# Fixing the order of weight splits and sums, and moving four steps, in the squared-ReLU MLP of an fp32 encoder layer

## The chip, the cores and the metric

The kernel runs on one core of a Trainium2 chip, as one program. The metric is the device time of one execution in microseconds; the median of three runs is 1119.77 us (1118.83 to 1120.58). The core has five engines with a queue each, which the profile names PE (TensorE; PEld is its weight load), DVE (VectorE), ACT (ScalarE), POOL (GpSimd) and SP (SyncE, which issues the transfers here).

## What is computed

One encoder layer in float32 for 256 tokens of width 2048: a mixer of two attention kinds, a cross attention over 256 memory tokens, and an MLP of width 8192, each followed by a layer norm of `alpha*x + f(x)`. The change touches only the MLP:

```python
def squared_relu_mlp(h, w_mlp_in, w_mlp_out):
    return jnp.square(jax.nn.relu(h @ w_mlp_in)) @ w_mlp_out
...
        ff = squared_relu_mlp(x, w_mlp_in[l], w_mlp_out[l])
        x = layer_norm(ALPHA * x + ff, ln3_g[l], ln3_b[l])
```

## The kernel before

**Products in three parts.** Every float32 operand is split in a high part, which TensorE's fast float32 form holds, and a low part, the remainder. `split` (L85) writes the high part with a ScalarE copy (L87) and the low part with a VectorE subtraction (L88). A product is then three matmuls (`mm3`, L152 to L155): high by high, high by low, low by high.

**The MLP in chunks.** The 8192 hidden columns are cut into NCH = 4 chunks of CH = 16 column tiles of 128. Chunk 0 of the hidden layer is made in four groups of four tiles (`hidden_group`, L944). From there on a mixed part runs: while the second product of chunk c goes on, the hidden columns of chunk c + 1 are made. The second product of a chunk goes in two halves q = 0, 1 of 1024 output columns, so there are eight passes (c, q), `PASSES` in the code, run by `one_pass` (L1011).

**Items.** The mixed part is a hand-written list `items` (L880 to L892) of two kinds. A tile item ("g", c + 1, j) makes one hidden column tile (`hidden_tile`, L965): two weight pieces of 1024 columns are split, 16 matmuls of 512 columns (L973) and 16 of 256 (L981) fill one PSUM bank, `evacuate` (L856) brings it to SBUF (ScalarE L858, VectorE L859), and after each second tile `finish` (L861) does relu and square (L863, L864), splits the pair, and for pairs 2 to 7 (`SEVEN`) forms four sums of its quarters (L874) and splits them too. A unit item ("u", c, q, p) multiplies hidden pair p (two blocks of 128 tokens by two of 128 hidden columns) with its 256 x 1024 piece of the output weights. In each half with q = 0 the first FIRST = 6 tiles stand one ahead of each of the first six units; with q = 1 the other ten stand one ahead of each unit and two ahead of each of the last two. The last chunk has units only.

**Sevens and plain units.** A plain unit takes eight block products into the four sum banks x11, x12, x21, x22. A seven takes seven products, some of sums of blocks, into x11, x12, x21 and the product banks p1, p5, p6, p7. It needs three sums of weight pieces on VectorE (`push_sums`, L913; the instructions are of L919), which go to the buffer s_t and are split from there. `SEVENS` and `ORDER` (L821 to L824) say which pairs of a pass are sevens and in which order the units go. In the last chunk's first half they are 4 to 7 of (0, 4, 1, 5, 2, 6, 3, 7), in its last half 5, 6, 7 of (0, 5, 6, 1, 7, 2, 3, 4). PSUM has eight banks and all are in use: the x banks are the page's "acc", the p banks its "att".

**Merges.** When a pass has done its last seven, p1 is copied to m_t (L1075), and eight VectorE steps (L1038, L1036 in the first chunk, and L1041) that merge the products into the residual `res` are put in `banks`; each weight piece then takes one of them off (`pump`), and the first seven of the next pass takes all that are left. The x banks are merged at the end of the pass. A tile ahead of a pass's first unit writes bank p6 (x22 in the first pass), tiles between the sevens write x22, tiles after them p1 and p7.

**Order of the work.** `part` (L925) splits one weight piece and then takes one sum, or else one side job, off its queue. The program is built by a tile framework that orders each engine's instructions itself, from an estimate of the time line (`schedule_with_timeline_sim=True`, L1270); program order is a guide, and only what `pin` (L82) marks keeps it. Weights come by SyncE in tiles of 1024 KB into four buffers in turn (`fetch`, L894, issue L908), one fetch at the start of each item. Split weights go to four high buffers and four low buffers.

**The end.** The last three units of the last pass (HELD = 3) first fill x12 and x11 for token block 0; their splits are kept and later serve block 1 in x21 and, in two quarters, two product banks. `done` (L1110) adds the banks to the residual and takes statistics; the layer norm of block 0, then block 1, follows on VectorE (L1145, L1153) with the output transfers (L1156).

Of the kernel before, what the change touches and what calls it, by code (L numbers as in the profile page):

```python
# [14 lines left out]
AF = mybir.ActivationFunctionType  # L15
ALU = mybir.AluOpType
# [17 lines left out]
CH = 16  # L34
# [4 lines left out]
def encoder_kernel(ctx: ExitStack, tc: tile.TileContext, t, out):  # L39
    nc = tc.nc  # L40
# [20 lines left out]
    def f(ap):  # L61
        return ap.bitcast(F32)
# [22 lines left out]
    def split(hi, lo, src, scale=None, pinned=False):  # L85
        if scale is None:
            pin(nc.scalar.activation(hi, src, AF.Copy), pinned)  # L87
            return pin(nc.vector.tensor_tensor(out=lo, in0=src, in1=f(hi), op=ALU.subtract), pinned)  # L88
        else:
            nc.scalar.activation(hi, src, AF.Copy, scale=scale)  # L90
            nc.vector.scalar_tensor_tensor(
                out=lo, in0=src, scalar=scale, in1=f(hi), op0=ALU.mult, op1=ALU.subtract)
# [7 lines left out]
        return r[:, :n]  # L100

    side, banks, fixed_lo = deque(), deque(), deque()

    def pump(n=1):

# [205 lines left out]
    class Heads:  # L311
# [11 lines left out]
        def finish(self):  # L323
            while self.live:
                self.step()
# [495 lines left out]
    ORDER = {cq: (2, 3, 4, 5, 6, 7, 0, 1) for cq in PASSES[:-2]}  # L821
    SEVENS = {cq: SEVEN for cq in PASSES[:-2]}
    ORDER[NCH - 1, 0], SEVENS[NCH - 1, 0] = (0, 4, 1, 5, 2, 6, 3, 7), (4, 5, 6, 7)
    ORDER[NCH - 1, 1], SEVENS[NCH - 1, 1] = (0, 5, 6, 1, 7, 2, 3, 4), (5, 6, 7)  # L824
    HELD = 3
    FIRST = 6
    s_in = Stream(t["w_mi"][4:])
    sts = [stats_tile() for _ in range(NB)]
    ht = big3("ht")
# [16 lines left out]
    def give(what, c, p):  # L846
        free[what].append(place[what, c, p])
# [31 lines left out]
    raws, raw_of, fetched, sums = [raw_x], {}, [0], deque()  # L879
    items = []  # L880
    for c, q in PASSES:
        gs = [("g", c + 1, j) for j in range(CH)] if c < NCH - 1 else []
        gs = gs[:FIRST] if q == 0 else gs[FIRST:]
        us = [("u", c, q, p) for p in ORDER[c, q]]
        n = len(gs) - len(us)
        for i, u in enumerate(us):
            twice = i >= len(us) - n if n > 0 else False
            for _ in range(2 if twice else 1):
                if gs:
                    items.append(gs.pop(0))  # L890
            items.append(u)
        assert not gs  # L892

    def fetch():  # L894

        n = fetched[0]
        if n == len(items):
            return
        it = items[n]
        fetched[0] += 1  # L900
        if n and n < 4:
            raws.append(raw_tile())
        raw = raw_of[it] = raws[n % 4]
        if it[0] == "g":
            src = t["w_mc"][(it[1] - 1) * CH + it[2]]
        else:
            src = t["w_mo"][(it[1] * 2 + it[2]) * (CH // 2) + it[3]]
        nc.sync.dma_start(raw, src)  # L908
# [4 lines left out]
    def push_sums(it):  # L913

        raw = raw_of[it]
        b12, b22, b21 = [raw[:, o:o + 512] for o in (0, 1024, 1536)]

        def add(out, a, b):
            sums.append(lambda: nc.vector.tensor_tensor(out=out, in0=a, in1=b, op=ALU.add))  # L919
        add(s_t[:, 0:1024].rearrange("p (i c) -> p i c", i=2), raw[:, 512:1536].rearrange("p (i c) -> p i c", i=2),  # L920
            b12[:, None, :].broadcast_to([P, 2, 512]))
        add(s_t[:, 1024:1536], s_t[:, 0:512], b22)
        add(s_t[:, 1536:2048], s_t[:, 1024:1536], b21)

    def part(src, hi=None, lo=None):  # L925
        w = src.shape[1]
        if hi is None:
            hi = wsp.tile([P, 1024], F32R, tag="w_hi", name="w_hi")
        if lo is None:
            lo = lo_tile()  # L930
        split(hi[:, :w], lo[:, :w], src)
        if banks:
            pump()
        if sums:
            sums.popleft()()
        else:
            pump()
        return hi[:, :w], lo[:, :w]
# [21 lines left out]
                evacuate(outs[i + j], l, h, j)  # L960
            finish(h, c, (j0 + i) // 2)

    lh = []

    def hidden_tile(it, ps):  # L965

        _, c, j = it
        for h_ in range(2):
            hi, lo = part(raw_of[it][:, h_ * 1024:(h_ + 1) * 1024])
            k0 = 8 * h_  # L970

            def w_hi(k):
                nc.tensor.matmul(ps, hi[:, k * P:(k + 1) * P], x2t[:, k0 + k, :],  # L973
                                 start=k0 + k == 0, stop=k0 + k == KT - 1)

            for k in range(7):
                w_hi(k)
            if h_ == 0:
                w_hi(7)
            for k in range(8):  # L980
                nc.tensor.matmul(ps[:, 0:S], lo[:, k * P:(k + 1) * P], x2t[:, k0 + k, 0:S],  # L981
                                 start=False, stop=False)
            if h_ == 1:
                w_hi(7)
        if j % 2 == 0:
            lh[:] = [tmp_tile(), tmp_tile()]
        evacuate(ps, *lh, j % 2)
        if j % 2:
            finish(lh[1], c, j // 2)

    bank = []
    at = [0]
# [1 line left out]
    def step():  # L994

        it = items[at[0]]
        at[0] += 1
        fetch()
        if at[0] < len(items) and not is_seven(it) and is_seven(items[at[0]]):
            push_sums(items[at[0]])  # L1000
        return it
# [9 lines left out]
    def one_pass(c, q):  # L1011
# [32 lines left out]
        while n_unit < len(order):  # L1044
            it = step()
            if it[0] == "g":
                if n_unit == 0:
                    ps = x22 if (c, q) == (0, 0) else p6
                elif n_seven < len(sevens):
                    ps = x22  # L1050
                else:
                    spare = spare or [p1, p7]
                    ps = spare[0]
                    spare.reverse()
                hidden_tile(it, ps)
                continue
            p, raw, k = it[3], raw_of[it], 2 * it[3]
            n_unit += 1
            if p in sevens:
                if n_seven == 0:  # L1060
                    while banks:
                        banks.popleft()()
                while sums:
                    sums.popleft()()
                for src, todo in ((raw[:, 512:1536], ((p1, a(c, k, 0)), (x12, sm(c, p, 3)))),
                                  (raw[:, 1536:2048], ((x11, a(c, k + 1, 0)),)),
                                  (s_t[:, 0:1024], ((p5, sm(c, p, 0)), (p7, sm(c, p, 2)))),
                                  (s_t[:, 1024:2048], ((p6, sm(c, p, 1)), (x21, a(c, k + 1, 1))))):
                    for (hi, lo), (ps, x) in zip(halves(part(src)), todo):
                        mm(ps, x, hi, lo)  # L1070
                n_seven += 1
                if at[0] < len(items) and is_seven(items[at[0]]):
                    push_sums(items[at[0]])
                if n_seven == len(sevens):
                    nc.scalar.activation(m_t, p1, AF.Copy)  # L1075

                    banks.extend([lambda: merge(r11, m_t), lambda: more(p6),
                                  lambda: merge(r12, m_t, ALU.subtract), lambda: more(p7),
                                  lambda: merge(r21, m_t), lambda: merge(r22, m_t, ALU.subtract),
                                  lambda: merge(r22, p5), lambda: merge(r12, p5)])  # L1080
            elif final and len(order) - n_unit < HELD:
                n = len(parts) // 2
                for i in range(2):
                    o = (2 * n + i) * 1024
                    lo = wide[:, 6144 + o:7168 + o] if n == 0 else aux[:, 2048 + o:3072 + o]
                    w = halves(part(raw[:, i * 1024:(i + 1) * 1024], wide[:, o:o + 1024], lo))
                    parts.append((k + i, w))
                    for (hi, lo), ps in zip(w, (x12, x11)):
                        mm(ps, a(c, k + i, 0), hi, lo)
            else:  # L1090
                for i in range(2):
                    w = halves(part(raw[:, i * 1024:(i + 1) * 1024]))
                    for (hi, lo), to in zip(w, ((x12, x22), (x11, x21))):
                        for b in range(2):
                            mm(to[b], a(c, k + i, b), hi, lo)
            if q == 1:
                give("h", c, p)
                if p in SEVEN:
                    give("s", c, p)
        if not final:  # L1100
            for r, ps in ((r22, x22), (r12, x12), (r11, x11), (r21, x21)):
                merge(r, ps)
            if c == NCH - 1:
                banks.extend([lambda b=b, r=r: stats(sts[b], r)
                              for b, r in ((0, r11), (0, r12), (1, r21), (1, r22))])
            return
# [167 lines left out]
```

## Time and profile before

| what | value |
|---|---|
| median of three runs | 1119.77 us |
| the profiled execution's own time | 1118.91 us |
| its span, first to last instruction | 1117.1 us |
| TensorE (PE) busy | 1085.0 us, 5855 matmuls |
| VectorE (DVE) busy | 949.0 us, 1344 instructions |
| ScalarE (ACT) busy | 641.6 us, 928 instructions |
| mean granted TensorE clock | 0.991 |
| read from HBM | 212.78 MB |

A row of the timeline reads: start in us from the span's start, duration, engine, source line, operation, tile written and tiles read, shapes, count, and in brackets the idle time before it with what ended it. A row of the stretches has its length, then each engine's busy time with its count of instructions, the granted clock (1.00 is full), the DMA engines' busy share and GB/s. In a row of waits stand the total, the count and the longest. In a row of groups stand the busy time, the mean duration in ns and the idle time before. The mixed part begins near 494 us with the first tile item, its last pass ends near 1101 us, and the final normalisation ends the kernel.

### The profile page before, as it was taken

The page shows a single profiled execution, that of the slowest core. Times are in us where ns is not written, and L with a number is a line of the kernel's source. Part 1 is how long each engine was busy: PE and PEld are TensorE (multiplying, and loading weights), DVE is VectorE, ACT ScalarE, POOL GpSimd, SP SyncE. Part 2 cuts the span into 40 slices and gives each one's busy share as a digit, 9 for nine tenths or more (in the row PEclk, how much of TensorE's full clock was granted, in tenths as well). Part 3 has the DMA queues.
Part 4 walks back from the last instruction along what each step waited for, and adds up shares of the span by engine and source line. Part 5 has one row for each costly group of instructions (what it writes and reads, how often), then busy time and mean ns, then how long its engine had stood idle before and what let it go on. Part 6 is the DMA issues. An engine that isn't in the chain of part 4 may idle for free.

```text
span 1117.1 us, 15372 instructions
## 1 busy us (share of the span) xinstructions
PE 1085.0 (97%) x5855; PEld 930.1 (83%) x5855; DVE 949.0 (85%) x1344; ACT 641.6 (57%) x928; POOL 38.2 (3%) x45
## 2 busy tenths in 40 slices
PE   9999999999999999999999999999999999999984
PEld 6988899888998878887878888878888878888763
DVE  5878677687888777898899988899989989988988
ACT  6555566546576345576657656566655655755540
POOL 1402000000100000000000000000000000000000
PEclk9999999999999999999999999999999999999987
DMA  9664454466477426654545655546565455564532
GB/s 327 234 226 151 152 189 141 162 226 238 177 226 263 153 76 226 221 195 158 219 177 200 219 196 188 219 159 226 188 212 192 182 205 190 188 226 170 207 140 87
DMA packets 37945, 215.87 MB, mean 193 GB/s; under 512 B 4336, under 2 KB 5232, under 8 KB 14192
## 3 DMA queue, kind: packets, MB, share of 16 engines
q1 hardware_dynamic: 37872, 214.89, 53.9%
q8 instruction: 46, 0.75, 0.3%
q14 instruction: 27, 0.22, 0.1%
HBM read 212.78 MB, written 2.10 MB: 192 GB/s over the span
## 4 chain that ended last, share of the span: by engine, by line
PE 88%; DVE 6%; DMA 2%; ACT 1%; issue 1%; SPq 0%; POOL 0%; DVEq 0%; ACTq 0%
PE acc L154 12%; PE acc L155 12%; PE acc L153 12%; PE acc L973 9%; PE att L973 6%; PE acc L981 5%; PE att L153 4%; PE att L154 4%; PE att L155 4%; PE att L981 3%; PE acc L202 3%; PE att L202 3%; PE acc L195 2%; PE acc L193 2%; PE acc L194 2%; DVE lo L88 2%
## 5 line engine op out<-in xcount | busy, mean ns | idle before, releaser
L87 ACT ACTIVATE w_hi<-raw 128x1024 fp32r<-128x1024 f32 (+2 forms) x320 | 305.1, 970 | 160.8 <-PE acc L155 90.3
L88 DVE TENSOR_TENSOR lo<-raw,w_hi 128x1024 fp32r<-128x1024 f32 (+1 forms) x190 | 206.5, 1101 | 8.7 <-ACT w_hi L87 7.7
L88 DVE TENSOR_TENSOR w_lo<-raw,w_hi 128x1024 fp32r<-128x1024 f32 (+2 forms) x130 | 146.0, 1132 | 59.2 <-ACT w_hi L87 58.2
L973 PE MATMUL acc<-x2t,w_hi 128*128 128x512 f32 x496 | 129.0, 392 | 0.2 <-DVE tmp L859 0.2
L88 DVE TENSOR_TENSOR lo<-s_t,w_hi 128x1024 fp32r<-128x1024 f32 x86 | 104.9, 1221 | 18.4 <-ACT w_hi L87 13.2
L87 ACT ACTIVATE w_hi<-s_t 128x1024 fp32r<-128x1024 f32 x86 | 90.7, 1056 | 42.5 <-PE acc L155 24.6
L973 PEld LDWEIGHTS acc<-x2t,w_hi 128*128 128x128 f32 x496 | 91.0, 189 | 17.5 <-ACT w_hi L87 0.6
L973 PE MATMUL att<-x2t,w_hi 128*128 128x512 f32 x272 | 70.4, 393 | 1.3 <-DVE m_t L1041 1.3
L981 PEld LDWEIGHTS acc<-x2t,lo 128*128 128x128 f32 x496 | 67.6, 190 | 4.7
L858 ACT ACTIVATE tmp<-acc 128x256 f32<-128x256 f32 x39 | 14.4, 384 | 97.5 <-PE acc L973 94.6
L154 PE MATMUL acc<-w_lo,xt 128*128 128x512 f32 (+2 forms) x192 | 69.6, 364 | 0.1
L155 PE MATMUL acc<-w_hi,xt 128*128 128x512 f32 (+2 forms) x192 | 69.6, 363 | 0.0
L981 PE MATMUL acc<-x2t,lo 128*128 128x256 f32 x496 | 69.1, 282 | 0.0
L88 DVE TENSOR_TENSOR lo<-raw_x,w_hi 128x1024 fp32r<-128x1024 f32 (+1 forms) x56 | 66.7, 1209 | 2.7 <-ACT w_hi L87 2.6
L153 PE MATMUL acc<-w_hi,xt 128*128 128x512 f32 (+2 forms) x192 | 66.3, 365 | 0.9 <-ACT w_hi L87 0.9
L154 PE MATMUL acc<-lo,ht 128*128 128x512 f32 x158 | 62.0, 392 | 2.4 <-DVE lo L88 2.4
L155 PE MATMUL acc<-w_hi,ht 128*128 128x512 f32 x158 | 61.6, 390 | 0.0
L87 ACT ACTIVATE w_hi<-raw_x 128x1024 fp32r<-128x1024 f32 (+1 forms) x56 | 57.4, 1046 | 4.8 <-PE att L973 1.5
L973 PEld LDWEIGHTS att<-x2t,w_hi 128*128 128x128 f32 x272 | 49.6, 189 | 11.4 <-DVE m_t L1041 2.7
L919 DVE TENSOR_TENSOR s_t<-s_t,raw 128x512 f32<-128x512 f32 x84 | 57.4, 684 | 0.1
L153 PE MATMUL acc<-w_hi,ht 128*128 128x512 f32 x158 | 54.9, 396 | 0.3 <-ACT w_hi L87 0.3
L919 DVE TENSOR_TENSOR s_t<-raw 128x1024 f32<-128x1024 f32 x42 | 51.3, 1222 | 1.5 <-DMA raw<-in_w_mo 0.8
(308 smaller groups left out, 2513.7 us busy)
## 6 DMA issues: line engine op xcount, KB each, us to landing
raw<-in_w_mo SPq DMA_DIRECT2D x54, 1024.0 KB, 4.9
raw<-in_w_mc SPq DMA_DIRECT2D x30, 1024.0 KB, 4.8
raw_x<-in_w_mc SPq DMA_DIRECT2D x18, 1024.0 KB, 4.9
raw<-in_w_out SPq DMA_DIRECT2D x16, 1024.0 KB, 4.9
raw<-in_w_mi SPq DMA_DIRECT2D x16, 1024.0 KB, 4.9
raw_x<-in_w_mo SPq DMA_DIRECT2D x10, 1024.0 KB, 4.9
raw<-in_w_b SPq DMA_DIRECT2D x5, 1024.0 KB, 4.9
raw<-in_w_qa SPq DMA_DIRECT2D x16, 256.0 KB, 5.4
```

Of the source, the lines that this page charges most:

```text
L87: pin(nc.scalar.activation(hi, src, AF.Copy), pinned)
L88: return pin(nc.vector.tensor_tensor(out=lo, in0=src, in1=f(hi), op=ALU.subtract), pinned)
L153: nc.tensor.matmul(ps, ah, bh, start=start, stop=False)
L154: nc.tensor.matmul(ps, ah, bl, start=False, stop=False)
L155: nc.tensor.matmul(ps, al, bh, start=False, stop=stop)
L193: nc.tensor.matmul(ps, hi, xt[:, k, 0:S], start=k == 0, stop=False)
L194: nc.tensor.matmul(ps, hi, xt[:, k, S:2 * S], start=False, stop=False)
L195: nc.tensor.matmul(ps, lo, xt[:, k, 0:S], start=False, stop=k == nk - 1)
L202: pin(nc.tensor.matmul(ps, hi[:, i * P:(i + 1) * P], xt[:, k, :], start=k == 0, stop=k == nk - 1), pinned)
L919: sums.append(lambda: nc.vector.tensor_tensor(out=out, in0=a, in1=b, op=ALU.add))
L973: nc.tensor.matmul(ps, hi[:, k * P:(k + 1) * P], x2t[:, k0 + k, :], start=k0 + k == 0, stop=k0 + k == KT - 1)
L981: nc.tensor.matmul(ps[:, 0:S], lo[:, k * P:(k + 1) * P], x2t[:, k0 + k, 0:S], start=False, stop=False)
```

## The change

Five edits, all in the mixed part.

- **Queued.** Each w_hi copy, each low subtraction of `part` and each sum of `push_sums` gets an order dependence on the one queued before it on the same engine. ScalarE so keeps program order among its weight copies, VectorE among its weight subtractions and sums. No semaphore is added; evacuations, finishes and merges are not queued.
- **Last half all plain.** The pass (3, 1) takes its eight units in order 0 to 7, none of them a seven.
- **Two tiles lead.** In the first pass (0, 0) two tile items stand ahead of the first unit, and seven instead of six in that pass; nine are left for (0, 1). The second tile writes p6.
- **Finish later.** The finish of a tile pair is put behind the next unit, or ahead of the next tile if that comes first.
- The construction of `items` is rewritten for this; from (1, 0) to (2, 1) it gives the same list as before.

```diff
+    queued = {}
+
+    def queue(ins):
+
+        i = ins.ins
+        if i.engine in queued:
+            tc.add_manual_dep(i, queued[i.engine], mybir.DependencyInfo(
+                mybir.DependencyClass.NoSync, mybir.DependencyReason.DATA), reason="queue")
+        queued[i.engine] = i.name
+        return ins
...
-    ORDER[NCH - 1, 1], SEVENS[NCH - 1, 1] = (0, 5, 6, 1, 7, 2, 3, 4), (5, 6, 7)
+    ORDER[NCH - 1, 1], SEVENS[NCH - 1, 1] = tuple(range(CH // 2)), ()
     HELD = 3
-    FIRST = 6
...
     for c, q in PASSES:
-        gs = [("g", c + 1, j) for j in range(CH)] if c < NCH - 1 else []
-        gs = gs[:FIRST] if q == 0 else gs[FIRST:]
         us = [("u", c, q, p) for p in ORDER[c, q]]
-        n = len(gs) - len(us)
+        if c == NCH - 1:
+            items += us
+            continue
+        lead = 7 if c == 0 else 6
+        gs = [("g", c + 1, j) for j in (range(lead, CH) if q else range(lead))]
+        twice = range(8 - (len(gs) - 8), 8) if q else range(lead - 6)
         for i, u in enumerate(us):
-            twice = i >= len(us) - n if n > 0 else False
-            for _ in range(2 if twice else 1):
-                if gs:
-                    items.append(gs.pop(0))
-            items.append(u)
-        assert not gs
+            n = 2 if i in twice else 1
+            items += gs[:n] + [u]
+            gs = gs[n:]
...
         def add(out, a, b):
-            sums.append(lambda: nc.vector.tensor_tensor(out=out, in0=a, in1=b, op=ALU.add))
+            sums.append(lambda: queue(nc.vector.tensor_tensor(out=out, in0=a, in1=b, op=ALU.add)))
...
-        split(hi[:, :w], lo[:, :w], src)
+        queue(nc.scalar.activation(hi[:, :w], src, AF.Copy))
+        queue(nc.vector.tensor_tensor(out=lo[:, :w], in0=src, in1=f(hi[:, :w]), op=ALU.subtract))
...
-    lh = []
+    lh, late_finish = [], []
...
         if j % 2:
-            finish(lh[1], c, j // 2)
+            late_finish.append(lambda h=lh[1]: finish(h, c, j // 2))
...
         at[0] += 1
+        if it[0] == "g" and late_finish:
+            late_finish.pop()()
         fetch()
...
                 if n_unit == 0:
-                    ps = x22 if (c, q) == (0, 0) else p6
+                    ps = x22 if it[1:] == (1, 0) else p6
...
                 if p in SEVEN:
                     give("s", c, p)
+            if late_finish:
+                late_finish.pop()()
```

## The prediction

> **What bounds the kernel now.** I read the page first, then the busy time by stretches, then the timeline of the mixed MLP part (from about 494 us on).
>
> ```profile
> span 1117.1 us, 15372 instructions
> ...
> PE 1085.0 (97%) x5855; PEld 930.1 (83%) x5855; DVE 949.0 (85%) x1344; ACT 641.6 (57%) x928; POOL 38.2 (3%) x45
> ...
> PE 88%; DVE 6%; DMA 2%; ACT 1%; issue 1%; SPq 0%; POOL 0%; DVEq 0%; ACTq 0%
> ```
>
> TensorE is busy nearly all the time and carries 88% of the chain that ended last. So a gain can only be TensorE work that goes or TensorE idle time that goes, and the change adds TensorE work. The busy time of each stretch (columns: length, PE, PEld, DVE, ACT, POOL, clock, DMA share, GB/s) says where there is idle time to win:
>
> ```profile
> 554.30:640.00 85.70, 84.46 (x422) 70.71 (x420) 82.20 (x109) 55.54 (x72) 0.00 (x0) 1.00 0.55 195
> 640.00:724.80 84.80, 84.80 (x440) 72.88 (x441) 75.75 (x94) 49.78 (x64) 0.00 (x0) 1.00 0.56 201
> ...
> 1063.50:1101.00 37.50, 32.70 (x148) 26.78 (x148) 32.11 (x42) 10.82 (x12) 0.00 (x0) 0.91 0.32 112
> ```
>
> From 640.0 to 724.8 TensorE never rests; the stretch before loses a little, with VectorE at 82.20 of 85.70; the end loses much, and there the clock fell to 0.91. Busy time hides part of a loss, because the end of a matmul is modelled, so I count starts. The pitch of a 512-column matmul at full rate comes from two starts that are 21 matmuls apart:
>
> ```profile
> 1005.04 0.39 PE L155 MATMUL acc<-w_hi,ht 128*128 128x512 f32 x1
> ...
> 1009.80 0.39 PE L155 MATMUL acc<-w_hi,ht 128*128 128x512 f32 x1
> ```
>
> 4.76 / 21 = 0.227 us. What lies beyond 0.227 per matmul is lost.
>
> **Last half all plain.** In the last half (3, 1) the three pairs 5, 6, 7 went by seven products and now go by eight. The loss there before:
>
> ```profile
> 1057.20:1074.30 17.10, 11.48 (x35) 0.80 0.31 116
> ```
>
> ```profile
> 1063.54 0.49 PE L153 MATMUL att<-w_hi,aux 128*128 128x512 f32 x1
> 1064.04 2.35 DVE L88 TENSOR_TENSOR wide<-raw,wide 128x1024 fp32r<-128x1024 f32 x2
> ...
> 1067.52 1.26 DVE L1038 TENSOR_TENSOR res<-res,att 128x512 f32<-128x512 f32 x2
> ...
> 1068.84 0.79 PE L153 MATMUL att<-w_hi,aux 128*128 128x512 f32 x1 [4.80 <-DVE res L1038]
> ...
> 1073.00 0.63 PE L154 MATMUL att<-lo,aux 128*128 128x512 f32 x1
> ...
> 1073.43 0.63 PE L155 MATMUL att<-w_hi,aux 128*128 128x512 f32 x1
> ```
>
> The first window row is TensorE alone: 35 matmuls in 17.10 us, where 35 x 0.227 = 7.9 would do: 9.2 us lost. Most of it is one wait: a seven-product of the last half needs the product banks (p1, p5, p6, p7, "att") that the previous half filled, and VectorE merges them into the residual (L1038) only after low parts of later units. After this idle time the pitch is 0.43 (1073.00 to 1073.43) instead of 0.227, and the window's clock is 0.80. [...]
>
> Plain units touch no product bank, so this wait has no cause left: -9.2. Price: a plain unit has 8 x 3 matmuls, a seven 7 x 3, so 3 x 3 x 0.227 = +2.0. What is late next is the merge of the four sum banks (x22, x12, x11, x21) at the boundary of the halves, which the plain units do need. Four such merges, two to 1.26 us by the row above, are 2.5; the last seven hides most of it, since x22 and x12 are finished before its last matmuls; I take +0.5 (bounds 0 and 2.5). The merges of the products now lie behind the plain units, and VectorE has room for them: the change takes these off it,
>
> ```profile
> L919 DVE TENSOR_TENSOR s_t<-s_t,raw 128x512 f32<-128x512 f32 x84 | 57.4, 684 | 0.1
> ...
> L919 DVE TENSOR_TENSOR s_t<-raw 128x1024 f32<-128x1024 f32 x42 | 51.3, 1222 | 1.5 <-DMA raw<-in_w_mo 0.8
> ```
>
> 3 x (2 x 0.68 + 1.22) = 7.7 us of sums, beside the splits of those sums and eight merges. Transfers: 1 MB per plain unit of 24 x 0.227 = 5.4 us is 193 GB/s (w_mo tiles are 1024 KB), and 640.0 to 724.8 moved 201 GB/s without a rest of TensorE; nothing. Together -6.7.
>
> **Splits and sums queued.** All w_hi copies on ScalarE, and all lo subtractions and sums (L919) on VectorE, now keep program order. What that repairs:
>
> ```profile
> 899.42 1.07 PE L153 MATMUL acc<-w_hi,ht 128*128 128x512 f32 x4
> 899.48 1.23 DVE L919 TENSOR_TENSOR s_t<-raw 128x1024 f32<-128x1024 f32 x1 [0.77 <-DMA raw<-in_w_mo]
> ...
> 900.62 1.22 DVE L88 TENSOR_TENSOR lo<-raw_x,w_hi 128x1024 fp32r<-128x1024 f32 x1
> ...
> 901.90 0.50 PE L154 MATMUL acc<-lo,ht 128*128 128x512 f32 x1 [1.41 <-DVE lo L88]
> ...
> 902.24 0.40 PE L155 MATMUL acc<-w_hi,ht 128*128 128x512 f32 x1
> ```
>
> A sum for the next half's first seven stands on VectorE ahead of the lo that TensorE needs at once, and even waits for its transfer. Four matmuls from 899.42 would let the next start at 900.33; it starts at 901.90, and the one after it comes 0.34 later instead of 0.227: 1.57 + 0.11 = 1.68 lost, 0.27 more than the idle time in brackets. The same pattern, shorter, stands at three places:
>
> ```profile
> 515.94 0.50 PE L154 MATMUL att<-lo,aux 128*128 128x512 f32 x1 [0.55 <-DVE lo L88]
> ```
>
> ```profile
> 560.03 0.50 PE L154 MATMUL acc<-lo,ht 128*128 128x512 f32 x1 [0.55 <-DVE lo L88]
> ```
>
> ```profile
> 730.53 0.50 PE L154 MATMUL acc<-lo,aux 128*128 128x512 f32 x1 [0.55 <-DVE lo L88]
> ```
>
> Each 0.55 + 0.27 = 0.82. In program order the sum comes behind the next tile's first lo: 1.68 + 3 x 0.82 = -4.1.
>
> The cost of a fixed order: where the lo at the head waits for its w_hi, a sum that was ready used to fill VectorE, and now stands behind it with every later lo; TensorE waits for those. What VectorE waits for in one chunk (554.3 to 724.8):
>
> ```profile
> DVE tmp L859 <- ACT tmp L858: 6.2, 6, 1.8
> DVE lo L88 <- ACT w_hi L87: 5.4, 13, 0.5
> ```
>
> Lower bound 0: merges, evacuations and finishes aren't queued and fill the hole, and the postponed finish (below) gives more of that. Upper bound: the 1.22 us first sum of each of 12 sevens per chunk becomes idle time, 14.6 us per chunk. I take +1.5 in all, near the lower end: the rows above are short waits (at most 0.5 us for a w_hi), and the stretch from 554.3 has only 3.5 us of VectorE idle time, so other work is there. On ScalarE (55.54 busy of 85.70) the order costs nothing.
>
> **Two column tiles first.** The first half opened tile, seven, tile. What it lost:
>
> ```profile
> 502.45:508.10 5.65, 4.32 (x13) 1.00 0.58 191
> ```
>
> ```profile
> 497.69 0.40 PE L973 MATMUL acc<-x2t,w_hi 128*128 128x512 f32 x1
> ...
> 498.95 0.74 DVE L859 TENSOR_TENSOR tmp<-att,tmp 128x256 f32<-128x256 f32 x2
> ...
> 508.16 1.20 PE L973 MATMUL acc<-x2t,w_hi 128*128 128x512 f32 x4 [0.19 <-DVE tmp L859]
> ```
>
> 13 matmuls in 5.65 us, 2.7 lost, waiting for splits of the seven (VectorE still finishes the last group of chunk 0), then for the evacuation of the one bank x22 that both tiles used. Now the second tile writes p6, and 32 more TensorE matmuls stand ahead of the first seven, for only two more lo. -2.7. But p6 is one of the "att" banks of the last group, and its evacuation ended at 499.69 (second row: 498.95 + 0.74), where the second tile would start at about 498, behind the last matmul of the first (first row). I take +0.7 back (bounds 0 and 1.7): -2.0. One tile fewer pads the half after it; its 16 tiles a chunk stay, so no sum changes.
>
> **Finish later.** The relu, square, split and sums of a finished tile pair go behind the unit that follows: four ScalarE and at most six VectorE instructions a pair, no DMA, nothing of GpSimd. Nothing reads them before the next chunk. The fetches on SyncE keep their number, and each still goes out at the start of an item. It moves VectorE work off a unit's lo, at 0 for TensorE by itself; it is the filler named above. These two waits of each chunk I leave as they are, since both come from banks and buffers that the change doesn't touch:
>
> ```profile
> 582.79 0.50 PE L153 MATMUL att<-w_hi,ht 128*128 128x512 f32 x1 [0.24 <-ACT w_hi L87]
> ```
>
> ```profile
> 639.99 1.19 PE L973 MATMUL att<-x2t,w_hi 128*128 128x512 f32 x4 [0.45 <-DVE m_t L1041]
> ```
>
> **The tail.**
>
> ```profile
> 1090.84 0.69 DVE L1041 TENSOR_TENSOR m_t<-m_t,att 128x512 f32<-128x512 f32 x1 [4.66 <-PE att L155]
> ...
> 1097.15 1.28 DVE L1111 TENSOR_TENSOR res<-res,acc 128x512 f32<-128x512 f32 x2
> ```
>
> Before the final additions of block 0 (L1111) VectorE merged the products of the last sevens, from 1090.84 to 1097. That goes. Block 0 can start as soon as its banks are complete; the held products of block 1 that follow are 18 of 512 and 36 of 256 columns, 18 x 0.227 + 36 x 0.12 (half the pitch, an estimate) = 8.4 us. So up to 4 us could move ahead of TensorE's end; but the rest is VectorE's own work in series, so I take -1.5 (bounds 0 and -4).
>
> **Sum.** -6.7 - 4.1 + 1.5 - 2.0 - 1.5 = -12.8. The profiled execution took 1118.91 (its span 1117.1), 0.86 under the median of 1119.77: 1106.1 on its footing, 1107.0 on the median's, which I give.
>
> **Rivals.**
> A. The queued order costs in the full halves: the three stretches like 554.3 to 640.0 have 3.5 us of VectorE idle time each for six sevens, six first sums are 7.3. If that excess of 3.8 shows on TensorE in each, +11.4 minus the 1.5 already taken: 1107.0 + 9.9 = 1117, still a little faster or the same. For it: VectorE at 96% there. Against: unqueued fillers.
> B. The queued order starves VectorE throughout, so the kernel is slower: for each of 40 sevens (43 less 3) more than 0.36 us of new TensorE idle time cancels the 12.8 + 1.5. At half a sum, 0.61 x 40 = 24: 1107.0 - 1.5 + 24 = 1130. For it: VectorE's queue has no way around a waiting lo. Against: the waits for w_hi above are 0.5 us at most.
> C. The long wait only moves to the start of the last half: VectorE does product merges before the sum banks or the lo. Eight merges of 0.63 = 5.0, with the slow clock after it about 7.5: 1107.0 + 7 = 1114. For it: that is the order it chose at 1064. Against: the plain lo are now in one queue.
> D. The waits at 582 and 640 go as well (about 0.5 and 0.7 with the 0.27, three times), the start gets no wait and the tail gives 3: 1107 - 3.6 - 0.7 - 1.5 = 1101.
>
> **Chances.** Forecast 0.52, A 0.17, B 0.08, C 0.11, D 0.12. Range 1100 to 1117: it holds all but B and the outer half of A. A measurement of this kernel can tell about 0.2% (2.2 us) from no change. Faster takes the forecast, C, D and most of A: 0.86; same, from A, 0.06; slower, B, 0.08.
>
> **What would show it.** Right: no TensorE wait on L1038 in the last half and a clock of 1.00 to its end; no L919 directly ahead of a lo that TensorE waits for; 9 more matmuls (5864); tile, tile, unit at 492 to 508 with under 1 us lost; the first L1111 further ahead of TensorE's end. Wrong: waits for lo in each unit of the middle halves with VectorE idle before them (A, B), or several us at the first unit of the last half (C).

## The result and the profile after

The changed kernel takes 1102.78 us (median; 1101.22 to 1104.22) against 1119.80 us: the ratio is 0.9848, with a 95% interval of 0.9831 to 0.9865, so 17 us or 1.5% faster. The profiled execution took 1102.56 us, its span 1100.6. The forecast was 1107.0 in a range of 1100 to 1117: the time lies inside the range, and each stretch in which the forecast put a gain shows one; the gain was a third larger than forecast (17.0 against 12.8).

From the page of the kernel after, the span, the busy times and the shares of the last chain:

```profile
span 1100.6 us, 15374 instructions
...
PE 1082.0 (98%) x5864; PEld 932.9 (85%) x5864; DVE 930.4 (85%) x1321; ACT 635.4 (58%) x921; POOL 38.3 (3%) x45
...
DVE 1%; issue 0%; DVEq 0%
```

TensorE has the nine matmuls more that were counted, VectorE 18.6 us less work. (The last chain breaks off here inside the tail, as its shares show, so nothing is read from it.) The stretches of the kernel after, with the columns as before:

```profile
502.45:508.10 5.65, 5.65 (x30) 4.83 (x29) 5.14 (x11) 5.30 (x10) 0.00 (x0) 1.00 0.39 164
...
554.00:640.00 86.00, 85.31 (x425) 71.41 (x425) 83.35 (x111) 53.76 (x69) 0.00 (x0) 1.00 0.56 197
640.00:724.00 84.00, 84.00 (x435) 72.03 (x434) 75.62 (x95) 50.08 (x66) 0.00 (x0) 1.00 0.58 207
...
1060.00:1088.90 28.90, 28.90 (x146) 24.64 (x144) 19.95 (x29) 6.80 (x8) 0.91 (x1) 1.00 0.25 91
```

At the start (first row) and in the last half (last row) TensorE never rests, and the clock stays at 1.00 where it was 0.80. Only the stretches like 554 to 640, the second halves of the chunks, still lose something. What TensorE waits for in them, from the waits on TensorE:

```profile
PE acc L163 <- ACT w_hi L940: 1.0, 2, 0.5
PE att L164 <- DVE lo L941: 0.7, 1, 0.7
PE acc L983 <- ACT w_hi L940: 0.4, 2, 0.2
```

The 4.8 us for the product banks (L1038) and the waits for m_t (L1041) are gone, and so are the four waits behind sums that the forecast named. But one of its signs, no sum directly ahead of a lo that TensorE waits for, fails at one place. VectorE, then TensorE, in chunk 0's second half:

```profile
588.79 0.68 DVE L928 TENSOR_TENSOR s_t<-s_t,raw 128x512 f32<-128x512 f32 x1
589.39 1.82 DVE L941 TENSOR_TENSOR lo<-raw,w_hi 128x1024 fp32r<-128x1024 f32 x2
```

```profile
590.66 0.50 PE L164 MATMUL att<-lo,ht 128*128 128x512 f32 x1 [0.67 <-DVE lo L941]
```

Here the queue itself puts the sum there: in program order the last sum of a seven comes just ahead of that seven's first lo. To see where the 16.5 us between the two spans went, I add up, over all starts of TensorE, what each took beyond the pitch (0.227 us for 512 columns, 0.119 for 256), by stretches; the tail runs from the end of the last matmul's pitch to the end of the span. Microseconds:

| kernel | 490 to 554 | 554 to 1003 | from 1003 | tail |
|---|---|---|---|---|
| before | 4.3 | 9.4 | 10.2 | 15.7 |
| after | 0.3 | 7.5 | 0 | 11.7 |
| e1 plain last half alone | 4.2 | 9.3 | 0.2 | 14.0 |
| e2 after, sevens back | 0.3 | 7.6 | 8.1 | 14.6 |
| e3 after, no queue | 0.3 | 8.2 | 0.2 | 14.0 |
| e4 after, one tile leads | 7.0 | 8.0 | 0 | 11.7 |
| e6 queue alone | 7.0 | 8.0 | 7.8 | 14.5 |
| e10 leading tiles and late finish alone | 0.3 | 8.4 | 9.4 | 15.2 |
| e7 seven tiles in every first half | 0.3 | 3.5 | 0 | 11.7 |
| e8 four held units | 0.3 | 7.6 | 0 | 10.5 |
| e9 both | 0.3 | 3.7 | 0 | 10.5 |
| e12 both, no queue | 0.3 | 3.5 | 0.2 | 11.9 |

Before to after: -4.0 - 1.9 - 10.2 - 4.0, plus 2.0 for the nine matmuls (9 x 0.227), plus 1.5 that this one execution lost more in the unchanged part ahead of 490 us (16.2 against 14.7): -16.6. That 1.5 is the clock and not the change. TensorE has the same two idle times there in both kernels, of 0.71 and 1.57 us, and then the clock fell in this execution alone: the next 16 matmuls took 3.77 us (401.31 to 405.08) instead of 2.22 (401.29 to 403.51). The same stretch before, then after:

```profile
400.00:405.00 5.00, 4.71 (x29) 4.22 (x30) 3.95 (x9) 2.12 (x5) 0.00 (x0) 1.00 0.05 11
```

```profile
400.00:405.00 5.00, 4.70 (x19) 4.17 (x20) 3.43 (x8) 1.32 (x3) 0.00 (x0) 0.66 0.08 10
```

The profiled executions of e2, e4, e5 and e8 have this fall too (clock 0.66, 0.68, 0.67 and 0.68); the others do not. So the traces are compared below by stretches.

### The profile page after: what moved, and what is told of

Same layout as the page of the kernel before. It is cut to its first block, busy times and chain, and to the rows that moved or that the text cites. A ratio compares the mean times of both kernels' runs of the same rounds, so it can differ in the third digit from the quotient of the medians.

```text
span 1100.6 us, 15374 instructions
## 1 busy us (share of the span) xinstructions
PE 1082.0 (98%) x5864; PEld 932.9 (85%) x5864; DVE 930.4 (85%) x1321; ACT 635.4 (58%) x921; POOL 38.3 (3%) x45
## 5 line engine op out<-in xcount | busy, mean ns | idle before, releaser
L87 ACT ACTIVATE w_hi<-raw 128x1024 fp32r<-128x1024 f32 (+2 forms) x158 | 156.6, 999 | 125.7 <-PE acc L165 73.5
L941 DVE TENSOR_TENSOR lo<-raw,w_hi 128x1024 fp32r<-128x1024 f32 (+1 forms) x162 | 175.7, 1106 | 11.5 <-PE att L991 6.7
L940 ACT ACTIVATE w_hi<-raw 128x1024 fp32r<-128x1024 f32 (+1 forms) x162 | 151.6, 964 | 44.6 <-PE acc L165 27.1
L941 DVE TENSOR_TENSOR lo<-s_t,w_hi 128x1024 fp32r<-128x1024 f32 x80 | 97.5, 1220 | 13.9 <-ACT w_hi L940 11.9
L940 ACT ACTIVATE w_hi<-s_t 128x1024 fp32r<-128x1024 f32 x80 | 84.4, 1055 | 29.0 <-PE acc L165 20.9
L941 DVE TENSOR_TENSOR lo<-raw_x,w_hi 128x1024 fp32r<-128x1024 f32 (+1 forms) x56 | 64.4, 1161 | 7.0 <-ACT w_hi L940 3.4
L165 PE MATMUL acc<-w_hi,ht 128*128 128x512 f32 x164 | 63.8, 389 | 0.0
L940 ACT ACTIVATE w_hi<-raw_x 128x1024 fp32r<-128x1024 f32 (+1 forms) x56 | 54.7, 1007 | 9.7 <-PE acc L165 7.8
L163 PE MATMUL acc<-w_hi,ht 128*128 128x512 f32 x164 | 56.0, 390 | 0.5 <-ACT w_hi L940 0.5
L165 PE MATMUL acc<-w_hi,ot 128*128 128x512 f32 (+1 forms) x136 | 51.9, 382 | 0.0
```

The source lines that it names most:

```text
L163: nc.tensor.matmul(ps, ah, bh, start=start, stop=False)
L165: nc.tensor.matmul(ps, al, bh, start=False, stop=stop)
L940: queue(nc.scalar.activation(hi[:, :w], src, AF.Copy))
L941: queue(nc.vector.tensor_tensor(out=lo[:, :w], in0=src, in1=f(hi[:, :w]), op=ALU.subtract))
```

## The experiments

Each is timed in five rounds beside the kernel before; the ratio is to it.

**e1: the plain last half alone.** The kernel before with

```diff
-    ORDER[NCH - 1, 1], SEVENS[NCH - 1, 1] = (0, 5, 6, 1, 7, 2, 3, 4), (5, 6, 7)
+    ORDER[NCH - 1, 1], SEVENS[NCH - 1, 1] = tuple(range(CH // 2)), ()
```

> The kernel before with one edit: the last half all plain. Theory (each edit takes away its own wait): the wait on the product banks and the slow clock after it go, about 9 us, 9 matmuls come back as 2 us, and the tail loses the 4 us that it lost in the change, so about 1109 us; the waits at 502 and at 515, 560, 730 and 902 us stay. Rival (the queued order does most of it, the plain half alone moves the wait to its start): 1116 us or more, with several us of TensorE waiting for a merge or a lo in the last half.

Measured: 1109.6 us, 0.9917 (0.9905 to 0.993). The stretch from 1050 to the end of TensorE's work in e1, then the first addition of block 0 and the last matmul:

```profile
1050.00:1092.80 42.80, 42.80 (x207) 36.14 (x205) 31.53 (x41) 12.32 (x13) 0.91 (x1) 1.00 0.38 138
```

```profile
1086.31 1.37 DVE L1111 TENSOR_TENSOR res<-res,acc 128x512 f32<-128x512 f32 x2 [7.70 <-PE acc L155]
```

```profile
1092.78 0.28 PE L155 MATMUL att<-wide,aux 128*128 128x256 f32 x1
```

No wait, full clock: the plain half needs no queue. The rival falls. The tail shrank by 1.7 us, not by 4: the first addition stands 6.6 us ahead of TensorE's end (1092.9 - 1086.3), 4.3 in the kernel before. This edit alone is over half of the change.

**e2: the sevens back.** The kernel after with the old `ORDER` and `SEVENS` of the last half.

> The kernel after with the three sevens of the last half put back in their old order. Theory: 7 to 8 us of the wait and the clock and 4 us of the tail come back, about 1114 us. Rival (the queue alone keeps later lo from passing the merges, so the wait is short and the saved matmuls pay): 1104 us or less.

Measured: 1109.81 us, 0.9919 (0.9906 to 0.9933), between the two. TensorE in the last half of e2:

```profile
1058.55 0.50 PE L163 MATMUL att<-w_hi,aux 128*128 128x512 f32 x1 [0.58 <-ACT w_hi L940]
1060.97 0.50 PE L163 MATMUL att<-w_hi,aux 128*128 128x512 f32 x1 [1.92 <-DVE res L1050]
...
1062.70 0.80 PE L164 MATMUL att<-lo,aux 128*128 128x512 f32 x1 [0.53 <-DVE lo L941]
1063.30 0.63 PE L165 MATMUL att<-w_hi,aux 128*128 128x512 f32 x1
1063.73 0.63 PE L164 MATMUL acc<-lo,aux 128*128 128x512 f32 x1
```

The rival is right in part: with the queue the wait for the product banks falls from 4.80 to 1.92 us (without it, in e10, it stays at 4.80), as it should if low parts of later units can no longer pass the merges. But the waits around it (two more stand earlier, 1.46 us at 1052.52 and 0.68 at 1055.34) and the half rate after them (0.43 from 1063.30 to 1063.73) leave 8.1 of the 10.2 us.

**e3: no queue.** The kernel after without the dependences:

```diff
-        if i.engine in queued:
+        if False:
```

> The kernel after without the order dependences, the other edits kept. Theory: sums again stand ahead of a lo that TensorE needs, 3 places of 0.8 us and one of 1.7, less the 1.5 us of waits that the queue brought to the second halves: 1105 to 1107 us. Rival (the plain last half needs the queue too): 1110 us or more, with new waits after 1000 us.

Measured: 1105.12 us, 0.9878 (0.9864 to 0.9891): the queue is worth 2.3 us, about as the theory had it, but only in part for its reason. VectorE and TensorE of e3 at the end of chunk 0's first half, then the first addition of block 0 and the last matmul:

```profile
559.96 1.22 DVE L928 TENSOR_TENSOR s_t<-raw_x 128x1024 f32<-128x1024 f32 x1
...
561.10 1.22 DVE L941 TENSOR_TENSOR lo<-raw,w_hi 128x1024 fp32r<-128x1024 f32 x1
...
562.37 0.50 PE L164 MATMUL acc<-lo,ht 128*128 128x512 f32 x1 [0.93 <-DVE lo L941]
```

```profile
1082.22 1.37 DVE L1125 TENSOR_TENSOR res<-res,acc 128x512 f32<-128x512 f32 x2 [7.71 <-PE acc L165]
```

```profile
1088.70 0.28 PE L165 MATMUL att<-wide,aux 128*128 128x256 f32 x1
```

The sum ahead of the lo is back, and TensorE waits for it at the end of each chunk's first half (562, 726 and 897 us). But the other waits of the second halves are smaller without the queue, so in the middle it is worth 0.7 us (8.2 against 7.5). The larger part is the tail, 14.0 against 11.7: the first addition stands 6.6 us ahead of TensorE's end, as in e1. Together with 0.2 in the last half that is more than the 2.3 of the medians; by the traces the kernel after gives 1.1 of it back ahead of 490 us, where its clock fell and that of e3 did not.

**e4: one tile leads.** The kernel after with `lead = 6` for every chunk.

> The kernel after with one column tile ahead of the first seven, as before; queue, late finish and plain last half kept. Theory: 2 to 3 us of waits come back between 500 and 510 us, 1105 to 1106 us. Rival (the queue had already cured the start): within 0.7 us of the kernel after.

Measured: 1108.76 us, 0.9906 (0.9891 to 0.9921). Both expectations were too small: the second tile is worth 6 us. VectorE, then TensorE, at the start of e4:

```profile
502.98 1.22 DVE L928 TENSOR_TENSOR s_t<-raw 128x1024 f32<-128x1024 f32 x1
...
504.52 1.22 DVE L941 TENSOR_TENSOR lo<-raw,w_hi 128x1024 fp32r<-128x1024 f32 x1
...
506.26 0.69 DVE L928 TENSOR_TENSOR s_t<-s_t,raw 128x512 f32<-128x512 f32 x1
...
507.06 0.69 DVE L928 TENSOR_TENSOR s_t<-s_t,raw 128x512 f32<-128x512 f32 x1
507.66 1.82 DVE L941 TENSOR_TENSOR lo<-raw,w_hi 128x1024 fp32r<-128x1024 f32 x2
```

```profile
508.94 0.73 PE L164 MATMUL att<-lo,ht 128*128 128x512 f32 x1 [2.86 <-DVE lo L941]
509.47 0.63 PE L165 MATMUL att<-w_hi,ht 128*128 128x512 f32 x1
509.89 0.63 PE L164 MATMUL acc<-lo,aux 128*128 128x512 f32 x1
```

The second tile again waits for bank x22, so TensorE goes on to the next seven; but on VectorE the fixed order keeps that seven's lo (507.66) behind the tile's lo and all three sums. TensorE idles 1.04 us (at 505.06, for a w_hi) and then 2.86 us, and works at half rate after that (0.42 from 509.47 to 509.89). In the kernel before, VectorE could take that lo earlier: 4.3 us lost there, 7.0 here.

**e5: one tile leads, finish at once.** As e4, and

```diff
-            late_finish.append(lambda h=lh[1]: finish(h, c, j // 2))
+            finish(lh[1], c, j // 2)
```

> The kernel after with one tile ahead of the first seven and the finish of a tile pair at once, so of the change only the queue and the plain last half are left. Theory (the 3 us wait at the start with one tile comes from the queued order, since the second tile must wait for bank x22 and the unit behind it has its low parts last in the queue): the wait stays, 1108 to 1110 us. Rival (the late finish takes VectorE's place there): 1105 us or less, with the wait at 506 gone.

Measured: 1109.4 us, 0.9903 (0.9883 to 0.9922), with the same 3.1 us step at the start: the late finish isn't its cause, and has no effect of its own that this can tell (e4: 0.9906). It is what lets seven tiles stand in the first half, though: by the code, the second half then opens with the eighth tile, whose immediate finish would take an eighth place for sums before the first unit gives one back, and `free["s"]` has seven.

**e6: the queue alone.** The kernel before with the `queue` lines of the change and nothing else.

> The kernel before with the order dependences alone. Theory: about 2 us less in the middle halves, 2 less in the last half, 1 in the tail, and 3 more at the start, 1117 to 1119 us. Rival (the queue by itself gives what the forecast gave it, 4.1 less 1.5): 1116 us or less with no new wait at the start.

Measured: 1117.4 us, 0.9983 (0.9969 to 0.9997). The table shows why it is worth so little: what the queue gains in the middle, in the last half and in the tail (1.4, 2.4 and 1.2 us) it gives back at the start (2.7). The theory holds.

**e10: the leading tiles and the late finish alone.** The kernel after with the edits of e2 and e3.

> The kernel after without the queue and with the sevens of the last half back, so only the two leading tiles and the late finish are left of the change. Theory (the tiles repair the start by themselves, the other places stay as before): the 4.2 us of the start go, 1115 us. Rival (without the queue the first tiles do not get VectorE's place): 1118 us or more with waits of 2 us or more between 490 and 515 us.

Measured: 1113.21 us, 0.9953 (0.9937 to 0.997). TensorE in the first half of e10, and in its last half:

```profile
494.00:554.00 60.00, 60.00 (x314) 51.54 (x314) 55.27 (x73) 41.10 (x57) 0.00 (x0) 1.00 0.53 196
```

```profile
1063.61 0.80 PE L163 MATMUL att<-w_hi,aux 128*128 128x512 f32 x1 [4.80 <-DVE res L1050]
```

The tiles repair the start by themselves, and the 4.80 us wait stands as in the kernel before. About 6 us came in all: beside the start's 4.0, 1.0 in the middle (8.4 against 9.4), 0.8 in the last half and 0.5 in the tail.

**e7: seven tiles in every first half.** The waits left in the kernel after, at the start of the second half of chunk 1, TensorE and then VectorE:

```profile
743.98 0.50 PE L163 MATMUL acc<-w_hi,aux 128*128 128x512 f32 x1 [0.49 <-ACT w_hi L940]
...
746.55 2.11 PE L983 MATMUL acc<-x2t,w_hi 128*128 128x512 f32 x8 [0.22 <-ACT w_hi L940]
```

```profile
738.92 0.68 DVE L1050 TENSOR_TENSOR res<-res,acc 128x512 f32<-128x512 f32 x1
739.51 1.28 DVE L1050 TENSOR_TENSOR res<-res,att 128x512 f32<-128x512 f32 x2
740.71 0.68 DVE L1050 TENSOR_TENSOR res<-res,acc 128x512 f32<-128x512 f32 x1
741.31 0.68 DVE L928 TENSOR_TENSOR s_t<-s_t,raw 128x512 f32<-128x512 f32 x1
741.91 1.82 DVE L941 TENSOR_TENSOR lo<-raw,w_hi 128x1024 fp32r<-128x1024 f32 x2
```

Merges of the half before stand ahead of the unit's sum and lo. In the kernel before, VectorE took that lo ahead of these merges (at 741.69, the merges from 744.03). What ended the wait at 743.98 is a high part that ScalarE wrote from 742.88, behind an evacuation; TensorE had no lo to go on with in the meantime. So e7 moves one tile of each later chunk from the second half to a place between the last seven and the plain units of the first:

```diff
-        lead = 7 if c == 0 else 6
+        lead = 7
-        twice = range(8 - (len(gs) - 8), 8) if q else range(lead - 6)
+        twice = range(8 - (len(gs) - 8), 8) if q else range(c == 0)
```

> The kernel after with seven tiles in the first half and nine in the second for every chunk, the seventh tile between the last seven and the plain units (chunk 1's first half keeps two in front). Theory (the waits at 584 to 594, 743 to 757 and 913 to 927 us come from merges that pile up on VectorE at the start of a second half, and a tile ahead of the plain units gives VectorE 2.5 us more there): most of their 5.3 us goes, 1098 to 1101 us. Rival (VectorE's load moves on with the tile): no change within 1.5 us, with new waits later in the second halves.

Measured: 1096.37 us, 0.979 (0.9767 to 0.9812), more than expected. Two second halves in e7, and the one wait that is left, in the chunk whose list did not change:

```profile
724.00:810.00 86.00, 86.00 (x440) 73.52 (x439) 83.45 (x111) 53.53 (x71) 0.00 (x0) 1.00 0.55 199
895.00:980.00 85.00, 85.00 (x431) 72.54 (x430) 82.11 (x108) 52.03 (x68) 0.00 (x0) 1.00 0.60 210
```

```profile
588.47 0.50 PE L164 MATMUL att<-lo,ht 128*128 128x512 f32 x1 [0.66 <-DVE lo L941]
```

VectorE is as busy as before (83 of 86 us), and TensorE doesn't wait: VectorE's load did not make these waits. That the place of its merges did is the likely reading, but not shown by itself, since the moved tile also shifts ScalarE's copies. 4.0 us of the 6.4 stand in the table and are the edit's; 2.2 more (16.2 against 14.0) are the part ahead of 490 us, 1.5 of it the fall of the clock at 400 us.

**e8: four held units.** The kernel after with HELD = 4; the fourth unit's splits stay in the ordinary buffers.

```diff
-    HELD = 3
+    HELD = 4
...
+                    kept = ()
+                    if n < 3:
+                        kept = (wide[:, o:o + 1024],
+                                wide[:, 6144 + o:7168 + o] if n == 0 else aux[:, 2048 + o:3072 + o])
+                    w = halves(part(raw[:, i * 1024:(i + 1) * 1024], *kept))
```

> The kernel after with four held units at the end instead of three, so that 11.2 us instead of 8.4 of TensorE's work lies behind the sums of token block 0. Theory (the tail shrank because VectorE's chain of additions and normalisation begins earlier before TensorE's end): the first L1125 addition stands about 11.7 us instead of 8.85 before TensorE's end and the tail is 1 to 1.5 us shorter, since block 1's own chain then bounds it. Rival (the tail shrank because VectorE has no product merges left): no difference.

Measured: 1100.26 us, 0.9824 (0.9801 to 0.9847). The first addition (here L1128) and the last matmul of e8:

```profile
1076.76 1.37 DVE L1128 TENSOR_TENSOR res<-res,acc 128x512 f32<-128x512 f32 x2 [6.34 <-PE acc L165]
```

```profile
1088.31 0.28 PE L165 MATMUL att<-w_hi,aux 128*128 128x256 f32 x1
```

11.7 us apart (1088.4 - 1076.8), and the tail is 10.5 against 11.7 us: as the theory had it; the rival falls. The time alone can't tell e8 from the kernel after, since the intervals overlap; the trace can.

**e9, e11 and e12: both, and two variants.** e9 has the edits of e7 and e8. e11 moves the tile ahead of the last seven of the very first half behind it; e12 is e9 without the dependences.

```diff
-            n = 2 if i in twice else 1
+            n = 2 if i in twice else (c, q, i) != (0, 0, 5)
```

> Seven tiles in every first half and four held units together. Theory (the two gains lie at different places): 1094 us, 2 us under the seven tiles alone, tail 10.5. Rival (the earlier end meets another bound in the tail): 1096 us.

> As seven tiles and four held units together, but in the very first half the tile ahead of its last seven is moved ahead of the plain unit after it, as in the other chunks. Theory (the wait that is left at 587 us comes from merges at the start of the second half, which this tile gives room for): 1.5 us less than without, 1092 to 1093 us. Rival (two sevens in a row starve TensorE of low parts there): 1095 us or more, with a new wait near 545 us.

> Seven tiles and four held units without the order dependences. Theory (the queue gains by keeping sums behind low parts and by the order of the held units' splits at the end): waits behind sums come back at the ends of first halves and the first L1125 addition comes later relative to TensorE's end, 3 to 5 us more than with the queue. Rival (with more slack the queue is no longer needed): within 1 us of it.

Measured: e9 1095.58 us, 0.9791 (0.9777 to 0.9804); e11 1096.02, 0.9794 (0.9781 to 0.9808); e12 1097.96, 0.9812 (0.9798 to 0.9826). e9 has the 10.5 us tail of e8; its time can't be told from e7's, but both are below the kernel after. In e11 the wait at 587 us goes (0.5 instead of 2.1 us lost in that half), but a loss of the same size comes ahead of it (2.3 instead of 0.3 us from 490 to 554), as the rival had it, though for a high part and not a low one:

```profile
552.17 0.50 PE L163 MATMUL att<-w_hi,sums_x 128*128 128x512 f32 x1 [1.27 <-ACT w_hi L940]
```

e12 loses 2.4 us on e9, less than expected. One lo stands behind a sum again, at 562 us, but the middle as a whole loses no more than in e9 (3.5 against 3.7); what the trace shows is 1.4 in the tail and 0.2 in the last half. The wait at 562:

```profile
561.86 0.50 PE L164 MATMUL acc<-lo,ht 128*128 128x512 f32 x1 [0.92 <-DVE lo L941]
```

## Why the prediction was right, and where its sizes were off

**Last half: -6.7 forecast, -8.2 in the trace.** The mechanism is shown from both sides: e1 (the edit alone) takes the wait and the slow clock away (1.00 from 1050 to 1092.8), e2 and e10 (all but the edit) keep them (waits of 1.92 and 4.80 us, and a pitch of 0.43 after both). 10.2 us went and 2.0 came back as matmuls; the forecast's stretch held 9.2 of the 10.2, and the wait of 0.5 at the boundary did not come.

**Queue: -4.1 + 1.5 forecast.** The four waits behind sums were named rightly: all are gone with the queue alone (e6), 3.7 us. Without it three stand again in e3 and one in e12; the one at 515 also goes with the leading tiles alone (e10). But "these two waits of each chunk I leave as they are" failed both ways. The one at 640 and its like went, 1.8 us in the three chunks (two of the three are back in e3). The one at 582 and its like, 1.2 us in all, grew to 3.9 (0.66 + 0.39 and smaller ones in each of two chunks, 1.0 in the first), and e6 has such waits in every chunk with the queue alone: the price of the order was 2.7 us, not 1.5. The sign named above fails here too: the lo that TensorE lacks stands directly behind a sum (588.79 and 589.39, and 741.31 and 741.91 under e7). That the net of the queue's places, -1.9 in the middle and -0.7 at 515, came out at the forecast's -2.6 is in part luck: a gain that was left out paid for the larger price. The experiments also correct the sum's form: terms were added as if each edit stood alone. The queue alone is worth 0.17% (e6) because it makes the start worse, 7.0 us lost instead of 4.3; with the two leading tiles it is worth 2.3 us (e3). What the rivals A and B feared, TensorE starved by the fixed order, happened at that one place, which the change itself covers.

**Two tiles first: -2.0 forecast, with -0.8 of the queue's share at 515; -4.0 in the trace.** The wait for p6 (+0.7) did not come (0.3 us lost from 490 to 554). Beside the queue the tile is worth 6 us (e4); without the queue the tiles repair the start just as well (e10).

**Late finish: 0 forecast.** e5 against e4 agrees; its part is to make room for the seventh tile.

**The tail: -1.5 forecast, bounds 0 and -4; -4.0 in the trace.** This is the term that was most mis-sized, and the larger half of the error. Rightly seen was that VectorE's series from block 0's first addition to the end sets the tail, and that merges of the last sevens held it up: without them and without the queue (e1) the tail is 14.0, 1.7 less than before. What the sum put at nothing is the queue's part, another 2.3 (14.0 in e3, 11.7 after). The tail follows how far that first addition stands ahead of TensorE's end: 4.3 us before, 5.7 in e2 and e6, 6.6 in e1 and e3, 8.9 after and 11.7 in e8; the tails are 15.7, 14.6 and 14.5, 14.0, 11.7 and 10.5. In the kernel after that addition is TensorE's to release:

```profile
1080.06 1.37 DVE L1125 TENSOR_TENSOR res<-res,acc 128x512 f32<-128x512 f32 x2 [8.15 <-PE acc L165]
...
1088.82 0.28 PE L165 MATMUL att<-wide,aux 128*128 128x256 f32 x1
...
1096.38 0.88 DVE L1167 SCALAR_TENSOR_TENSOR res<-res,rs_r,raw_x 128x256 f32<-128x256 f32 x2
```

VectorE had been idle for 8.15 us when the banks came. The 8.9 us are the 8.4 that block 1's products need by the forecast's own count, and half a microsecond: nothing of them is done early. Without the queue some are. In e3 VectorE takes low parts of held units (written to `wide` and `aux`) ahead of a plain unit's, and TensorE takes block 1's products of 256 columns (into "att") in between:

```profile
1059.89 1.22 DVE L941 TENSOR_TENSOR wide<-raw,wide 128x1024 fp32r<-128x1024 f32 x1
1061.03 1.22 DVE L941 TENSOR_TENSOR lo<-raw,w_hi 128x1024 fp32r<-128x1024 f32 x1
1062.16 1.23 DVE L941 TENSOR_TENSOR lo<-raw_x,w_hi 128x1024 fp32r<-128x1024 f32 x1
```

```profile
1064.97 0.28 PE L163 MATMUL att<-wide,ht 128*128 128x256 f32 x1
```

In e1 and e3 19 of these 36 matmuls start before block 0's first addition; 19 x 0.119 = 2.3 us, the whole step from 8.9 to 6.6. In the kernel after and in e6, the queue alone, none does. So the queue shortens the tail by leaving TensorE all of block 1's work to do behind block 0. Why the framework places those matmuls early when the low parts come early is not shown.

Rival C (the wait moves to the start of the last half) did not happen. Of rival D, the larger tail, the start without a wait and the waits at 640 came; those near 582 did not go until e7, and there not in the first chunk.

## What to carry to other kernels

A fixed order repairs a queue only where the next work in that order can run; where TensorE is sent around a blocked item, the same order starves it (e4: 7.0 us lost at the start instead of 0.3), so a change of order and a bank for the item that blocks belong together and are to be costed together. When an engine at 97% waits in small pieces, look at what its feeders do just ahead of each wait, and move independent work there (e7: 4 us at an unchanged load of VectorE). The last vector chain starts where the first output's banks are complete, so give the matrix engine's other outputs the last place, whole (the tail is 14.0 us in e3, 11.7 in the kernel after, 10.5 in e8).

## What the runs showed of the hardware

TensorE's half rate, a pitch of 0.42 to 0.43 us instead of 0.227, stood not only behind the wait of 4.80 us: in e4 it followed waits of 1.04 and 2.86 us within 5 us (0.42 from 509.47 to 509.89), and in e2 waits of 0.58, 1.92 and 0.53 within 5 us (0.43 from 1063.30 to 1063.73), though TensorE worked between them. The single waits of 1.41 us before the change and 1.27 us in e11 left the rate whole (0.23 from 902.24 to 902.47, and from 552.75 to 552.98). The length of the waits does not settle it: the same 0.71 and 1.57 us near 400 us left the rate whole in the profiled execution before (four matmuls of 512 columns from 401.76 to 402.68, 0.23 each) and halved it in the one after (four from 402.12 to 403.83, 0.43 each), and no run here shows what decides. After the wait of 4.80 us in the kernel before, the half rate still held at 1073.43 (0.42 to the next start), 4.6 us after TensorE went on; from 1074.41 the pitch was 0.23. So a wait under 4.80 us did not always cost only itself: in e4 the six matmuls from 508.94 to 511.60 took 2.66 us, where 6 x 0.227 = 1.36 would do. And it need not be one wait: in e4 and e2 the idle time came in pieces, none over 2.86 us.
